# A two-layer hybrid attention encoder on one core: large element-wise operations leave POOL, and PE gets filler matmuls

## The chip, the cores and the metric

The kernel runs on 1 core of one Trainium2 chip. The metric is device time in microseconds (us) of one execution, as the median of the runs shown. The engines are PE (TensorE, matmuls and transposes), ACT (ScalarE), DVE (VectorE), POOL (GpSimd) and SP (which here only issues DMAs).

## The reference, cut to what matters

Two sequences (1024 and 512 tokens, each behind 16 meta tokens) pass through two layers. A layer is a root-mean-square norm, one wide input projection, rotary embedding, a windowed attention (A) with a sink term, a differential attention (B: softmax minus lambda times a second softmax), gates, an output projection, a second norm and the residual add.

```python
h = rmsnorm(x, pre_g)
proj = jnp.einsum('bld,de->ble', h, w_in)            # 1024 -> 3328
aq, ak, av, ag, bq, bk, bv, bg = parts
oa = window_gqa_attention(rope(aq), rope(ak), av, sink) * silu(ag)
ob = diff_attention(rope(bq), rope(bk), bv, lam, lambda_init, subln_g) * silu(bg)
o = jnp.einsum('ble,ed->bld', concat(oa, ob), w_out)  # 1024 -> 1024
return x + rmsnorm(o, post_g)
```

All tensors are float32.

## The kernel before

The 1568 token columns (1040 + 528) stand on the free axis in four chunks of 392 (`CH`), model features on the 128 partitions. A projection (`dense`) multiplies weights and activations that are each split into a rounded part and a rest: three matmuls for each 128 features, so 24 matmuls of up to 392 columns for an output of the input projection. The splitting is what makes so many large element-wise operations: for each weight block `load_w` copies 128x1024 into the rounded half and subtracts to get the rest; `prenorm` does the same for each row of each chunk; `project` does it for rotary results (`st`); `load_mix` does it for the attention results.

The order of the work is planned. Each call of the program is recorded as an operation (`Recorder`, `Engine.form`) with a cost for each engine that may do it, and `schedule` then plays a list schedule: whenever an engine is free it takes the ready operation of the highest priority, subject to buffers (PSUM: `ps_s` 1 buffer, `ps_t` 2, `ps_o` 1, `ps_d` 2). In the plan POOL and those DVE operations that read two SBUF operands exclude each other (`held`). `emit` then issues the operations in the planned order, so that each engine has a fixed queue, and the framework adds the semaphore waits. A planned time is used only for the order.

Where an operation may run on DVE or on POOL it is recorded by `any_tt`: the plan gives it to whichever of the two is free first. These are the weight rests (tile `whl`, also `kk`, `vv`, 128x1024), the prenorm products and rests (`at`, `slot`), the rotary products and sums (`ru`, `rw`, `t`, `st`), the combination of the two softmaxes in attention B (`pp`, up to 1040 columns), the residual adds (`slot`), the sums of squares, and two smaller kinds: the rests of the last 16 keys (`split_rem`, tile `pad`, up to 64 elements) and the gates of attention A (`og`, 256 elements). Three things are on POOL by other calls: the squares of `prestats` with `only=True` (ACT or POOL), the small steps on the statistics (tile `sm`: scale, power -0.5) in `rstd_bc` and `attn_b`, and a memset.

A chunk at the border of two layers goes through `post` (statistics by `rstd_bc`, eight scalings, the residual add, sums of squares) and `pre` (`prenorm` of the next layer), and only then can its next input projection start. `rstd_bc` is PE transpose, DVE sum, two small POOL operations, PE transpose, copy. The last chunk of the last layer ends the kernel with the first half of the same chain.

Of the kernel before, what the change touches and what calls it, by code (L numbers as in the profile page):

```python
# [18 lines left out]
PSUM = bass.MemoryType.PSUM  # L19
# [106 lines left out]
ENG = ("PE", "ACT", "DVE", "POOL", "SP")  # L126
PE_COL = 0.0004453
PE_SWITCH = 0.39


def _size(pat, shape, kw):
# [36 lines left out]
class Buf:  # L168
    def __init__(self, shape, dt, pool, ap=None, space="SB"):
        self.shape, self.dt, self.pool, self.ap, self.space = tuple(shape), dt, pool, ap, space  # L170
        self.acc = []
        self.left = 0
        self.stream = None
        self.live = pool is None
# [55 lines left out]
def _real(x):  # L230
    return x.get() if isinstance(x, View) else x
# [6 lines left out]
class Recorder:  # L238
# [3 lines left out]
    def __init__(self, nc):  # L242
        self.ops = []
        self.group = None
        self.stream = "dense"
        self.boost = 0
        self.base = 0
        self.rnd = random.Random(SEED)
        self.extra = []
        self.last = None  # L250
        self.weight = 1
        self.tensor = Engine(self, "PE", nc.tensor)
        self.vector = Engine(self, "DVE", nc.vector)
        self.scalar = Engine(self, "ACT", nc.scalar)
        self.gpsimd = Engine(self, "POOL", nc.gpsimd)
        self.sync = Engine(self, "SP", nc.sync)
# [37 lines left out]
        return self.call([g[0] for g in got], got[0][1], got[0][2])  # L294

    def any_tt(self, out, a, b, op):
        return self.any((self.vector, "tensor_tensor", (out, a, b), dict(op=op)),
                        (self.gpsimd, "tensor_tensor", (out, a, b), dict(op=op)))

# [138 lines left out]
        return order  # L438

    def emit(self):  # L440
        for o in self.schedule():
            for b in o.new:
                b.ap = b.pool.tile(b.shape, b.dt)
            for fn, args, kw in o.calls:
                fn(*[_real(a) for a in args], **{k: _real(a) for k, a in kw.items()})  # L445


class Pool:
# [9 lines left out]
class Engine:  # L458
# [3 lines left out]
    def form(self, name, args, kw):  # L462
# [14 lines left out]
        elif self.eng == "PE":  # L477
# [10 lines left out]
            if src.shape[0] <= 64:  # L488
                cost += PE_SWITCH
        elif self.eng == "ACT":  # L490
# [46 lines left out]
def hymba_kernel(ctx, tc, xT, w_in, w_out, rope, masks, pre_g, post_g, sub_g, sink_b, sink_m, lam_in, yT):  # L537
    real = tc.nc
    nc = Recorder(real)
# [54 lines left out]
    def f32(ap):  # L594
        return ap.bitcast(F32)
# [25 lines left out]
    identr = const.tile([128, 128], F32R, name="ident")  # L621
    nc.scalar.activation(identr, mk[:, 0:128], AF.Copy)
    ident = f32(identr)
    mhalf = const.tile([128, 4], F32, name="mhalf")
    nc.vector.memset(mhalf, -0.5)
    scl = const.tile([128, 1], F32, name="scl")
# [792 lines left out]
    for i in range(2):  # L1419
        hi, lo = pair(F32R)  # L1420
        for j in range(4):
            g = preg[:, 0, 4 * i + j:4 * i + j + 1]
            x, n = xin[0][i][:, j], CH[0][1]
# [94 lines left out]
```

## Time and profile before

| | us |
|---|---|
| median of 3 runs | 1985.34 (1983.41 to 1994.87) |
| the profiled execution, its own time | 1988.96 |
| its span, first to last instruction | 1986.8 |
| PE busy | 1841.9 (93%) |
| DVE busy | 1509.0 (76%) |
| ACT busy | 1015.0 (51%) |
| POOL busy | 825.2 (42%) |
| mean granted TensorE clock | 0.972 of full |

Busy shares are means over the whole span. What a change is worth is read from the stage it falls in, by what engine is busy there and what the others wait for.

### The profile page before, as it was taken

What the parts mean: (1) busy time and instruction counts of PE and PEld (TensorE: products, weight loads), DVE (VectorE), ACT (ScalarE), POOL (GpSimd) and SP (SyncE); (2) the same over time, 40 slices, a digit from 0 to 9 for tenths busy, and PEclk for the clock granted to TensorE, in tenths of its full rate; (3) what the DMA queues carried; (4) which work ended last, traced back from release to release, by engine and by line L of the source; (5) the groups of instructions that cost most, each with busy time, mean ns of one, the idle gap of its engine ahead of it and who ended that gap; (6) DMA issues with size and microseconds to landing.
All of it is one profiled execution on the core that took longest, in us unless ns stands there. A gap on an engine that the chain in (4) does not pass through costs nothing. (4 is left out here: it accounts for less than half of the span.)

```text
span 1986.8 us, 33503 instructions
## 1 busy us (share of the span) xinstructions
PE 1841.9 (93%) x11424; PEld 1757.3 (88%) x11424; DVE 1509.0 (76%) x3043; ACT 1015.0 (51%) x2358; POOL 825.2 (42%) x833
## 2 busy tenths in 40 slices
PE   5899999999999998999966999999999999899995
PEld 4889989989999988998856999999999998899994
DVE  7858777787777797687986577777877859768768
ACT  3325445454544575576544355555545537547541
POOL 6634362352352351002788452452613513421157
PEclk8999999999999999999978999999999999999997
DMA  6253363443434665555442535445453464764453
GB/s 229 60 159 112 104 169 100 135 128 111 141 93 122 165 176 158 120 134 144 158 151 84 151 98 152 128 128 158 115 173 96 124 166 120 193 176 102 122 173 130
DMA packets 289012, 271.06 MB, mean 136 GB/s; under 512 B 91402, under 2 KB 266058, under 8 KB 288714
## 3 DMA queue, kind: packets, MB, share of 16 engines
q1 hardware_dynamic: 288842, 268.92, 48.1%
q8 instruction: 91, 1.49, 0.3%
q14 instruction: 79, 0.65, 0.1%
HBM read 147.43 MB, written 95.94 MB: 122 GB/s over the span
## 5 line engine op out<-in xcount | busy, mean ns | idle before, releaser
L445 PE MATMUL ps_d<-slot,whl 128*128 128x392 f32 (+2 forms) x5712 | 1180.6, 349 | 53.6 <-POOL slot L445 13.7
L445 PEld LDWEIGHTS ps_d<-slot,whl 128*128 128x128 f32 x5712 | 998.5, 191 | 71.1 <-POOL slot L445 17.1
L445 PE MATMUL ps_s<-kk,qq 128*128 128x264 f32 (+9 forms) x1496 | 286.0, 318 | 18.0 <-DMA BS<-st 4.1
L445 PE MATMUL ps_o<-at,vv 128*128 128x256 f32 (+6 forms) x1368 | 286.3, 308 | 11.1 <-DVE at L445 5.5
L445 DVE TENSOR_TENSOR at<-ps_t,at 128x256 fp32r<-128x256 f32 (+6 forms) x472 | 224.7, 480 | 75.1 <-ACT at L445 67.8
L445 ACT ACTIVATE pp<-ps_s,sm 116x1040 f32<-116x1040 f32 (+4 forms) x208 | 203.9, 980 | 149.2 <-DVE sm L445 138.6
L445 ACT ACTIVATE at<-ps_t 128x256 fp32r<-128x256 f32 (+12 forms) x430 | 183.1, 434 | 166.8 <-PE ps_t L445 153.2
L445 PEld LDWEIGHTS ps_s<-kk,qq 128*128 128x128 f32 (+4 forms) x1496 | 229.1, 184 | 42.0 <-issue 5.2
L445 DVE TENSOR_REDUCE sm<-ps_s 116x1 f32<-116x1040 f32 (+4 forms) x208 | 218.7, 1051 | 51.5 <-PE ps_s L445 48.6
L445 ACT ACTIVATE pp<-pp,sm 128x336 f32<-128x336 f32 (+5 forms) x339 | 201.2, 606 | 77.3 <-DVE sm L445 74.9
L445 PEld LDWEIGHTS ps_o<-at,vv 128*128 128x128 f32 (+1 forms) x1368 | 215.0, 189 | 21.0 <-DVE at L445 9.2
L445 PE MATMUL ps_t<-ident,pp 128*128 128x128 f32 (+4 forms) x1208 | 196.4, 271 | 4.3 <-DVE pp L445 3.1
L445 PEld LDWEIGHTS ps_t<-ident,pp 128*128 128x128 f32 (+4 forms) x1208 | 143.6, 137 | 18.2 <-DVE pp L445 2.9
L445 POOL TENSOR_TENSOR sm<-sm 128x2 f32<-128x2 f32 (+2 forms) x112 | 49.6, 443 | 263.7 <-DVE sm L445 263.1
L445 POOL TENSOR_TENSOR pad<-pp,pad 128x64 fp32r<-128x64 f32 (+5 forms) x121 | 36.2, 302 | 231.3 <-DVE pad L445 117.2
L445 POOL TENSOR_TENSOR pp<-pp 128x1040 f32<-128x1040 f32 (+4 forms) x36 | 75.1, 2085 | 125.3 <-ACT pp L445 125.2
L445 POOL TENSOR_TENSOR whl<-wraw,whl 128x1024 fp32r<-128x1024 f32 x40 | 97.6, 2440 | 64.6 <-ACT whl L445 31.7
L445 POOL TENSOR_TENSOR slot<-slot 128x784 f32<-128x784 f32 (+7 forms) x41 | 93.6, 2286 | 39.3 <-ACT slot L445 14.4
L445 DVE CUSTOM_DVE_ANT_0 pp<-ps_s,mk,nsinks 128x336 f32<-128x336 f32 (+2 forms) x192 | 97.5, 525 | 16.1 <-PE ps_s L445 15.0
L445 POOL TENSOR_TENSOR ru<-ru,rw 128x392 f32<-128x392 f32 (+1 forms) x60 | 66.5, 1112 | 58.4 <-DVE rw L445 47.2
L445 ACT ACTIVATE og<-ps_o 64x128 f32<-64x128 f32 (+4 forms) x248 | 66.0, 287 | 47.6 <-PE ps_o L445 30.4
L445 DVE CAST at<-ps_t 128x256 fp32r<-128x256 f32 (+10 forms) x138 | 70.2, 509 | 16.6 <-PE ps_t L445 12.8
(157 smaller groups left out, 2442.1 us busy)
## 6 DMA issues: line engine op xcount, KB each, us to landing
wraw<-in_w_in_dram SPq DMA_DIRECT2D x48, 512.0 KB
BS<-st SPq DMA_DIRECT2D x112, 196.0 KB
qq<-qq SPq DMA_DIRECT2D x144, 128.0 KB
qq<-AQ SPq DMA_DIRECT2D x96, 128.0 KB
BV<-st SPq DMA_DIRECT2D x28, 392.0 KB
wraw<-in_w_out_dram SPq DMA_DIRECT2D x20, 512.0 KB
slot<-in_x_dram SPq DMA_DIRECT2D x12, 784.0 KB
GT<-ru SPq DMA_DIRECT2D x48, 196.0 KB
```

Source lines behind the costliest of these rows:

```text
L445: fn(*[_real(a) for a in args], **{k: _real(a) for k, a in kw.items()})
```

## The change

`any_tt` gives an operation of more than 300 elements in each partition to DVE alone; smaller ones may still go to either. The plan is made anew from this, so the order on all engines may differ. Second, while it issues, `emit` looks at each PE operation that takes a fresh PSUM buffer: where the plan has PE idle for more than 1.0 us ahead of it, it first issues int((idle - 0.6) / 0.232) matmuls of 512 columns into that buffer, with the identity as weights and one column of the identity, repeated, as the moving operand. Nobody reads their result; the operation that follows overwrites the buffer.

```diff
+POOL_MAX = 300
+FILL_MIN = 1.0
+FILL_REST = 0.6
+FILL_ONE = 0.232
...
     def any_tt(self, out, a, b, op):
+        n = 1
+        for k in out.shape[1:]:
+            n *= k
+        if n > POOL_MAX:
+            return self.vector.tensor_tensor(out, a, b, op=op)
         return self.any((self.vector, "tensor_tensor", (out, a, b), dict(op=op)),
                         (self.gpsimd, "tensor_tensor", (out, a, b), dict(op=op)))
...
     def emit(self):
+        until = 0.0
         for o in self.schedule():
             for b in o.new:
                 b.ap = b.pool.tile(b.shape, b.dt)
+            if o.eng == "PE":
+                fresh = [b for b in o.new if b.space == "PSUM"]
+                if self.filler is not None and fresh:
+                    self.fill(fresh[0], o.t0 - until)
+                until = o.t1
             for fn, args, kw in o.calls:
                 fn(*[_real(a) for a in args], **{k: _real(a) for k, a in kw.items()})
+
+    def fill(self, buf, idle):
+        n = int((idle - FILL_REST) / FILL_ONE) if idle > FILL_MIN else 0
+        out = buf.ap if len(buf.shape) == 2 else buf.ap[:, 0]
+        eye = _real(self.filler)
+        for _ in range(n):
+            self.tensor.raw.matmul(
+                out[:, 0:512], lhsT=eye, rhs=eye[:, 0:1].to_broadcast([128, 512]), start=True, stop=True)
...
     nc.scalar.activation(identr, mk[:, 0:128], AF.Copy)
     ident = f32(identr)
+    nc.filler = identr
```

## Rows read from the trace of the kernel before

**Rows 1.** Busy time of each engine by stage; columns as in the head line.
```profile
core 0: us, PE busy (x) PEld busy (x) DVE busy (x) ACT busy (x) POOL busy (x), PEclk, DMA share, GB/s
0.00:110.00 110.00, 82.18 (x427) 77.06 (x428) 83.93 (x116) 40.11 (x68) 68.26 (x53) 0.92 0.44 138
110.00:950.00 840.00, 805.47 (x5123) 769.87 (x5122) 634.50 (x1403) 449.93 (x1093) 284.61 (x347) 0.99 0.49 133
950.00:1100.00 150.00, 111.64 (x555) 100.49 (x552) 122.89 (x137) 71.01 (x118) 128.43 (x90) 0.85 0.39 131
1100.00:1900.00 800.00, 780.86 (x4985) 752.50 (x4986) 599.40 (x1314) 430.97 (x1037) 289.56 (x305) 1.00 0.51 141
1900.00:1987.00 87.00, 61.72 (x340) 57.41 (x339) 68.26 (x77) 22.94 (x44) 54.34 (x41) 0.88 0.40 133
```

**Rows 2.** Who PE waited for: us in total, times, longest.
```profile
PE ps_t L445 <- POOL sm L445: 16.4, 6, 7.3
...
PE ps_d L445 <- POOL slot L445: 13.7, 8, 3.3
```

**Rows 3.** Groups of POOL, shapes apart: largest and last one over 300 elements.
```profile
L445 POOL TENSOR_TENSOR whl<-wraw,whl 128x1024 fp32r<-128x1024 f32 x40 | 97.6, 2440 | 64.6 <-ACT whl L445 31.7 <-DVE whl L445 29.0 <-DVE sm L445 3.3
...
L445 POOL TENSOR_TENSOR pp<-pp 128x784 fp32r<-128x784 f32 x1 | 2.2, 2205 | 0.0
```

**Rows 4.** Groups of DVE, shapes apart; the first reads PSUM, the others SBUF alone.
```profile
L445 DVE SCALAR_TENSOR_TENSOR ru<-ru,ps_d 128x392 f32<-128x392 f32 x40 | 22.2, 558 | 17.6 <-ACT ru L445 17.4
L445 DVE TENSOR_TENSOR ru<-ru,rw 128x392 f32<-128x392 f32 x30 | 28.7, 955 | 0.5
L445 DVE SCALAR_TENSOR_TENSOR slot<-slot,postg,rb 128x384 f32<-128x384 f32 x16 | 21.6, 1398 | 0.0
```

**Rows 5.** Timeline of DVE and POOL in the border of the layers.
```profile
1001.12 0.96 DVE L445 TENSOR_TENSOR slot<-slot 128x784 f32<-128x784 f32 x1
1004.12 2.88 POOL L445 TENSOR_TENSOR slot<-at,slot 128x392 fp32r<-128x392 f32 x1 [4.36 <-ACT slot L445]
1004.63 0.55 DVE L445 TENSOR_TENSOR t<-t,ru 128x392 f32<-128x392 f32 x1
1005.11 0.55 DVE L445 TENSOR_TENSOR at<-at,rb 128x392 f32<-128x392 f32 x1
1020.75 12.48 DVE L445 SCALAR_TENSOR_TENSOR slot<-slot,postg,rb 128x392 f32<-128x392 f32 x7 [0.30 <-ACT rb L445]
1041.07 0.39 POOL L445 TENSOR_SCALAR sm<-sm 98x4 f32<-98x4 f32 x1
1053.47 4.37 DVE L445 SCALAR_TENSOR_TENSOR slot<-slot,postg,rb 128x392 f32<-128x392 f32 x8
1053.64 5.21 POOL L445 TENSOR_SCALAR sm<-sm 98x4 f32<-98x4 f32 x1 [1.52 <-DVE sm L445]
1060.96 0.91 PE L445 MATMUL ps_t<-ident,sm 98*128 98x98 f32 x4 [7.32 <-POOL sm L445]
```

**Rows 6.** Timeline behind the last dense matmul, DVE and POOL side by side.
```profile
1975.61 2.61 DVE L445 TENSOR_TENSOR slot<-slot 128x384 f32<-128x384 f32 x2
1978.14 4.40 DVE L445 SCALAR_TENSOR_TENSOR slot<-slot,postg,rb 128x384 f32<-128x384 f32 x4
1982.58 1.23 DVE L445 TENSOR_TENSOR slot<-slot 128x384 f32<-128x384 f32 x1
```

**Rows 7.** All 13 stretches at half clock, their first, largest, last and sum; columns as rows 1.
```profile
37.50:51.20 13.70, 6.17 (x20) 5.05 (x21) 10.64 (x15) 3.21 (x6) 8.61 (x6) 0.50 0.18 55
...
1058.10:1075.20 17.10, 7.76 (x23) 6.43 (x24) 5.47 (x5) 7.78 (x12) 15.29 (x13) 0.50 0.26 95
...
1966.10:1986.80 20.70, 1.80 (x6) 1.00 (x6) 14.90 (x14) 0.86 (x2) 12.31 (x11) 0.50 0.39 144
sum 109.70, PE 63.31 PEld 55.98 DVE 70.51 ACT 37.73 POOL 70.23; mean PE 4.87 PEld 4.31 DVE 5.42 ACT 2.90 POOL 5.40
```

More of the change, by code (lines that the diff above doesn't have):

```diff
@@ L251, in __init__ @@
         self.weight = 1
+        self.filler = None
         self.tensor = Engine(self, "PE", nc.tensor)
```

## The prediction

> **What bounds the kernel now.** I read the busy times first: PE is busy 1841.9 us of the span of 1986.8, DVE 1509, POOL 825. A mean can hide a stage, so I cut the span where the work changes [rows 1]. In the two long stretches inside the layers (110 to 950, 1100 to 1900) PE is busy 96% and 98%: PE bounds them, DVE has a quarter of its time free (75 to 76% busy), and a faster side engine buys next to nothing there. At the three edges it is otherwise: the head (0 to 110) has PE busy 75%, the border of the layers (950 to 1100) 74%, the tail (1900 to 1987) 71%. In the border POOL is busy 128 of 150 us and DVE 123: the two side engines set the pace, not PE. The waits of PE say the same: its longest single kind is for the statistics on POOL, followed among others by operations on `slot` on POOL [rows 2]. The clock comes last: 13 stretches of 110 us together were granted 0.5 (1.2 of 2.4 GHz), and PE was busy 63.3 us in them [rows 7]. In each of those I opened, PE had been waiting before or while the clock fell; the largest begins in the wait of 7.32 us at 1053.6 to 1061.0 [rows 5, 7].
>
> **Part one: operations leave POOL.** By the groups of POOL with shapes apart, 375 operations have more than 300 elements in a partition and take 609 us (the first and the last of these groups: [rows 3]). Five at the head are squares that no `any_tt` records and that stay. So 370 move, about 598 us of POOL, some 222,500 elements in each partition. Price on DVE with POOL out of the way: 0.55 us for 392 elements, 0.96 for 784, so (0.96 - 0.55) / 392 = 1.05 ns an element; the next one starts about 0.48 us after the first (1004.63, 1005.11), so some 0.065 us of each is fixed [rows 5]. That makes 222,500 x 1.05 ns + 370 x 0.065 us = 258 us added to DVE.
>
> Against it stands what DVE loses to POOL today. An operation of DVE that reads a PSUM operand takes 558 ns for 392 columns; one that reads SBUF alone takes 955 ns on average, and one kind of 384 columns 1398 ns [rows 4]. In the timeline seven scalings that take 0.55 to 0.62 us alone stretch over 12.48 us, and the reverse is there too: a POOL operation of 392 elements takes 2.88 us while two on DVE run inside it [rows 5]. They take turns, they don't share. I compared every SBUF-only instruction of DVE with the median of its kind and size while POOL rests and summed the excess: 190 us, of which about 185 fall beside operations that move. So DVE becomes 1509 - 185 + 258 = 1582 us, 80% of the span. By stage (same sums): head 84 - 26 + 18 = 76; first long stretch 634 - 37 + 82 = 679 of 840 (81%); border 123 - 43 + 44 = 124; second long stretch 599 - 57 + 94 = 636 of 800 (80%); tail 68 - 24 + 18 = 62. At the edges DVE does POOL's share at no cost at all, and POOL's time on the chain goes.
>
> Border: DVE needs 124 us, PE 111.6, of which 27 are at half clock (would be 99). The busiest engine needs 124 of today's 150, so at most 26 us go. ACT, the transposes and the small POOL steps of the statistics stay in the chain and leave gaps: I take 16 (bounds 0 and 26). Tail: behind the statistics of the last chunk DVE's pieces (2.61 for two additions, 4.40 for four scalings, 1.23 for one addition) [rows 6] run from 1973.9 to 1983.8; with all of POOL's share they would need 4 products and 8 additions at 0.48 and 4 scalings at 0.55, about 7.9 us, so 2 us less. Ahead of that, 1961.9 to 1971, DVE and POOL block each other for another 3: 5 us (bounds 1 and 9). Head: DVE 8 us less, but loads and the first statistics are in the chain: 4 us (bounds 0 and 9). Long stretches: the cover is PE, and DVE rises to 81%. Where PE waits for a result that lies behind a large subtraction in DVE's queue it loses; where it waited for POOL (13.7 us in all for `slot` [rows 2]) it gains. I put this at a loss of 5 us (bounds: gain 15, loss 55; the loss is a rival below).
>
> **Part two: fillers.** Full clock in all 13 stretches would save 63.3 x about half = 30 us of PE at most, and nothing where PE isn't last: in the tail 1.8 us of PE are concerned. Inside the long stretches the share is 24 us, worth 11; in the head 10 us, worth 4, mostly beside a chain of statistics; the border's is in the sum above. Fillers exist only where the plan has a gap, while the trace's gaps partly come from delays that no plan knows: I take 8 us of these 15. Cost: PE is idle 125 us between its instructions, and 41 gaps exceed 1 us, 94 us together, the longest 7.32 [rows 5]. Were the plan's gaps the same, (94 - 41 x 0.6) / 0.232 = 300 fillers would run. One in a gap costs nothing; one that runs when the next operation is ready delays it by its own length, twice that at half clock; and a filler can't start before its PSUM buffer is free, so where the gap is a wait for the buffer it falls behind the gap. Bounds: 0 and 69 us of delay; most gaps at the edges wait for data, not for a buffer, so I take 0 net beyond the 8.
>
> **Sum.** -16 - 5 - 4 + 5 - 8 = -28 us. The profiled execution took 1988.96 us (span plus 2.2), 3.6 above the median of the runs. So 1961 in its terms, 1957 against the median 1985.34.
>
> One rule stands against me. The Trainium skill, "SBUF — State Buffer" (Who interferes with whom), says that POOL and a DVE operation with two SBUF inputs contend for one pair of ports, held for a whole instruction while the other fully blocks. The rows agree: 12.48 us for seven scalings, and 5.21 us for a POOL step that takes 0.39 elsewhere. By that rule the small POOL steps that stay wait longer behind a fuller DVE; this is the second rival, priced from rows.
>
> **Rivals.** (a) The plan has few gaps where the chip has them: no fillers to speak of, the 8 us of clock are missing and part of the border's: 1966. (b) The statistics starve. At 1053.64 a POOL step of 0.39 us lasts 5.21 because eight scalings on DVE run back to back beside it, and PE then waits 7.32 us [rows 5]. Each of the 8 statistics in the border has two such steps; if 4 of the 16 lose 4.8 us on the chain, 19 us of the border's and tail's 21 are gone: 1976. For it: it happens today with POOL full. Against it: DVE's total in the border doesn't rise. (c) Fillers delay: a third of the 69 us falls where operands are ready or buffers late, 23 us: 1980. Against it: the gaps are mostly waits for data. (d) The other side, slower: DVE becomes the bound inside the layers. Some 235 of the moved operations fall there, 0.48 to 1.13 us each (mean 0.75), in a queue served in order, ahead of copies from PSUM of which PE has only two buffers of a kind. If PE sees none, nothing; if it sees 16% of them, the gain of 28 is gone; at 30% it is 53 us: 2010. For it: by the same sums over slices of 50 us, DVE would be busy 46 to 48 us in four of them. Against it: the mean there is 81%, and the plan puts copies ahead by priority. (e) More than the sum: the border shrinks to DVE's 124 us, the tail by 9, the head by 9, PE loses 15 us of waits inside the layers and the clock gives 15: 1985 - 74 = 1911 at the end, 1928 for about three quarters of it.
>
> **How the numbers follow.** About 1% (20 us) is what a measurement of this kernel tells from no change; the three runs shown differ by 0.6%. Chances: forecast 0.56 (its own range 1938 to 1968), (a) 0.10, (b) 0.10, (c) 0.07, (d) 0.07, (e) 0.10. Faster by over 1% (below 1965.5): 0.50 of the forecast, 0.06 of (a), all of (e): 0.66. Slower by over 1%: (d), 0.07. The rest, 0.27, is within 1%. The range runs from 1930, which holds (e) in part, to 1990, which leaves out (d).
>
> **What would show it.** Right: POOL's busy time near 230 us, DVE's near 1580; scalings of 384 columns near 600 ns; the stage between the layers nearer 130 than 150 us; PE waits for `slot` on POOL gone; fewer stretches at half clock; PE instructions above 11424 by some hundreds. Wrong: POOL's statistics still at several us with PE behind them (b), fillers running while the next operands are long done (c), PE waiting for DVE inside the layers at a busy share of DVE near 90% (d).

## The result, and the profile after

The changed kernel took 1967.01 us (median of 4 runs, 1965.23 to 1969.37) against 1987.88 us of the kernel before on the same chip: a ratio of 0.9893, 95% interval 0.9858 to 0.9927. The forecast was 1957 us, 28 us below the median known then; the measured gain is 21 us. The profiled execution has a span of 1967.4 us. Medians here and below leave out four slow executions of the kernels compared, of 2112 to 3605 us.

The page of the changed kernel, its engines and the granted clock in 40 slices:

```profile
PE 1870.9 (95%) x11646; PEld 1778.6 (90%) x11646; DVE 1551.1 (79%) x3384; ACT 1013.7 (52%) x2364; POOL 271.3 (14%) x486
...
PEclk9999999999999999999999999999999999999999
```

222 matmuls are fillers (11646 - 11424). POOL's busy time fell by 554 us and DVE's rose by only 42. The stages of [rows 1] again:

```profile
core 0: us, PE busy (x) PEld busy (x) DVE busy (x) ACT busy (x) POOL busy (x), PEclk, DMA share, GB/s
0.00:110.00 110.00, 100.57 (x549) 94.60 (x550) 83.84 (x154) 42.34 (x70) 20.65 (x22) 1.00 0.54 165
110.00:950.00 840.00, 808.31 (x5157) 768.07 (x5156) 671.10 (x1511) 445.02 (x1096) 123.43 (x250) 1.00 0.49 133
950.00:1100.00 150.00, 129.94 (x691) 119.75 (x690) 127.76 (x216) 71.78 (x119) 26.29 (x18) 0.97 0.44 142
1100.00:1900.00 800.00, 780.33 (x4968) 748.14 (x4967) 615.51 (x1410) 438.74 (x1048) 93.74 (x188) 1.00 0.50 137
1900.00:1987.00 87.00, 51.80 (x288) 48.05 (x286) 52.84 (x95) 15.78 (x32) 7.19 (x8) 0.93 0.38 127
```

Windows at fixed times no longer hold the same work, so I cut both spans at marks: the first score matmul of layer one (on `ps_s`), its last, the first of layer two, the last. From each length I also take the columns that PE's own matmuls stream in it, at the plan's own figure of 0.4453 ns each (`PE_COL`), because the new plan moves dense work from the edges into the layers. "Rest" is what is left of the length. Worked out from the timelines, one profiled execution of each kernel (executions of one kernel differ by up to 4 us after and 13 before, so a difference of 2 or 3 us in one stage is no more than a hint):

```
             before          changed         difference
stage        length  rest    length  rest    length   rest
head          132.8  46.7     117.2  33.7     -15.6  -13.0
layer one     801.8 119.8     814.9 118.3     +13.1   -1.5
border        198.8  69.3     175.4  64.2     -23.4   -5.1
layer two     734.4  88.1     748.3  92.2     +13.9   +4.1
tail          119.1  34.1     111.7  30.3      -7.4   -3.8
```

The groups of DVE that answer to [rows 4], of the changed kernel:

```profile
L461 DVE SCALAR_TENSOR_TENSOR ru<-ru,ps_d 128x392 f32<-128x392 f32 x40 | 22.3, 558 | 13.4 <-ACT ru L461 12.9
...
L461 DVE TENSOR_TENSOR ru<-ru,rw 128x392 f32<-128x392 f32 x80 | 42.9, 556 | 0.0
...
L461 DVE SCALAR_TENSOR_TENSOR slot<-slot,postg,rb 128x384 f32<-128x384 f32 x16 | 9.3, 613 | 0.0
```

The operation that reads PSUM is as long as before, 558 ns. The two that read SBUF alone fell from 955 to 556 and from 1398 to 613. Summed as in the prediction, DVE's excess over its undisturbed lengths fell from 190 to 11 us. Where the last chunk ends, the timeline reads (against [rows 6]):

```profile
1956.43 1.97 DVE L461 TENSOR_TENSOR slot<-slot,rb 128x384 f32<-128x384 f32 x4 [2.37 <-ACT rb L461]
1958.32 1.96 DVE L461 TENSOR_TENSOR slot<-slot 128x384 f32<-128x384 f32 x4
1960.19 2.20 DVE L461 SCALAR_TENSOR_TENSOR slot<-slot,postg,rb 128x384 f32<-128x384 f32 x4
1962.31 1.96 DVE L461 TENSOR_TENSOR slot<-slot 128x384 f32<-128x384 f32 x4
```

Sixteen operations in 7.8 us, with nothing of POOL between them; before, DVE and POOL together needed 9.9.

### The profile page after: what moved, and what is told of

Read it like the earlier page. It is cut to its first block, busy times and chain, and to the rows that moved or that the text cites. A ratio compares the mean times of both kernels' runs of the same rounds, so it can differ in the third digit from the quotient of the medians.

```text
span 1967.4 us, 33819 instructions
## 1 busy us (share of the span) xinstructions
PE 1870.9 (95%) x11646; PEld 1778.6 (90%) x11646; DVE 1551.1 (79%) x3384; ACT 1013.7 (52%) x2364; POOL 271.3 (14%) x486
## 5 line engine op out<-in xcount | busy, mean ns | idle before, releaser
L461 PE MATMUL ps_d<-slot,whl 128*128 128x392 f32 (+2 forms) x5712 | 1165.4, 346 | 16.6 <-DVE slot L461 9.9
L461 PEld LDWEIGHTS ps_d<-slot,whl 128*128 128x128 f32 x5712 | 985.6, 189 | 30.2 <-DVE slot L461 12.9
L461 ACT ACTIVATE at<-ps_t 128x256 fp32r<-128x256 f32 (+9 forms) x435 | 187.7, 440 | 180.4 <-PE ps_t L461 169.2
L461 POOL TENSOR_TENSOR pad<-pp,pad 128x64 fp32r<-128x64 f32 (+3 forms) x143 | 47.2, 332 | 793.3 <-ACT pad L461 494.3
L461 POOL TENSOR_TENSOR sm<-sm 128x2 f32<-128x2 f32 (+3 forms) x112 | 53.1, 475 | 480.7 <-DVE sm L461 467.1
L461 DVE TENSOR_TENSOR slot<-slot 128x784 f32<-128x784 f32 (+8 forms) x74 | 81.5, 1117 | 9.1 <-ACT slot L461 8.8
L461 DVE TENSOR_TENSOR whl<-wraw,whl 128x1024 fp32r<-128x1024 f32 x62 | 76.5, 1234 | 8.3 <-ACT whl L461 7.8
L461 POOL TENSOR_SCALAR sm<-sm 128x2 f32<-128x2 f32 (+6 forms) x72 | 51.8, 719 | 185.5 <-DVE sm L461 180.6
L461 ACT ACTIVATE pad<-pp 128x64 fp32r<-128x64 f32 (+5 forms) x144 | 33.4, 236 | 82.9 <-DVE pp L461 79.2
L461 DVE CAST at<-ps_t 128x256 fp32r<-128x256 f32 (+11 forms) x133 | 65.0, 489 | 12.9 <-PE ps_t L461 10.5
```

## The experiments

**One part alone.** First the new plan without fillers:

```diff
-FILL_MIN = 1.0
+FILL_MIN = 1e9
```

> The plan and the order of the changed kernel, without a single filler. Theory A (the prediction's split, scaled to the 21 us measured): leaving POOL gives about two thirds, fillers one third: about 1974 us. Rival B (the fillers carry the gain, since PE's busy time at half clock fell from 63 to 19 us): about 1984 us, near the kernel before. Rival C (fillers delay real work more than the clock gives back): 1967 us or less.

It took 1969.5 us, ratio 0.9903 (0.9882 to 0.9924), between theory A's 1974 and rival C's 1967. Leaving POOL is nearly the whole gain. The ratio with fillers, 0.9893, lies inside this interval, so whether fillers gain anything in this plan isn't shown. The other half alone, fillers in the plan of before:

```diff
-POOL_MAX = 300
+POOL_MAX = 1000000
```

> The plan and the order of the kernel before, with fillers in its gaps. Theory A: about 1980 us (8 us of clock). Rival B: about 1970 us. Rival C: at or above the 1988 us of before, since the plan that shares work with POOL is the less exact one and its fillers hit ready work.

1993.9 us, ratio 1.0020 (1.0004 to 1.0036): a trifle slower. Theory A's fillers and rival B both fall; C holds in this plan. Since both fillerless kernels issue the same order as their partners, I could follow each matmul through both. In the plan of before, the kernel with fillers gains 4.3 us in the head, loses 9.8 in layer one, gains 3.6 in the border, loses 4.3 in the rest. In the new plan it gains 2.4 in the head and 2.0 in the border and loses 2.7 in layer one. Not all of this is the fillers' doing: of the 9.8 us, some 2.6 are lost at each of two fills (at 405 and 788 us) and stay lost, and the rest builds up between fills.

The clock is not why: it did what was hoped. PE's busy time at half clock, all such stretches together, first the new plan without fillers, then with them:

```profile
sum 86.00, PE 52.91 PEld 48.49 DVE 65.91 ACT 34.21 POOL 14.40; mean PE 4.81 PEld 4.41 DVE 5.99 ACT 3.11 POOL 1.31
```

```profile
sum 29.80, PE 18.82 PEld 17.52 DVE 22.23 ACT 9.17 POOL 5.66; mean PE 3.14 PEld 2.92 DVE 3.71 ACT 1.53 POOL 0.94
```

34 us less of PE at half clock should be worth 17 us; the medians moved by 2.5. Of the 34, 19 lie in the border, where the granted clock of 950 to 1100 rose from 0.86 to 0.97, and 11 in the head; cut at the marks, these two stages became only 4.4 us shorter. What a filler can cost is seen at one place in layer one, here in the changed kernel:

```profile
573.54 1.23 DVE L461 TENSOR_REDUCE sm<-ps_s 116x1 f32<-116x1040 f32 x1
574.80 1.13 ACT L461 ACTIVATE pp<-ps_s,sm 116x1040 f32<-116x1040 f32 x1 [1.78 <-DVE sm L461]
...
576.07 3.42 PE L469 MATMUL ps_s<-ident 128*128 128x512 f32 x8 [2.56 <-ACT pp L461]
```

and in the kernel without fillers:

```profile
575.81 2.08 PE L461 MATMUL ps_s<-kk,qq 128*116 128x264 f32 x6 [2.54 <-ACT pp L461]
```

The gap is a wait for the only `ps_s` buffer, which ACT still reads. Eight fillers wait for that buffer too, start at its end and run 3.42 us, nearly all at half clock (0.50 from 575.6 to 579.0), while the real matmul, ready at 576.1 here and started at 575.8 without them, starts at 579.3. But this loss doesn't last. The kernel with fillers ran 0.2 us behind the other just before this place, 3.5 at it, and 0.5 again at 600: behind the fillers the real work ran at full clock, where without them it was at half (575.2 to 582.1). The lasting part of the 2.7 us came earlier, from 265 to 290 us, where the last filler lay 220 us back. There PE waited 2.00 us for DVE in the changed kernel and the granted clock fell to 0.50 (271.8 to 275.2); without fillers the same wait was 0.23 us and the clock stayed full:

```profile
271.53 2.14 PE L461 MATMUL ps_d<-slot,whl 128*128 128x392 f32 x6 [2.00 <-DVE rw L461]
```

```profile
273.55 1.34 PE L461 MATMUL ps_d<-slot,whl 128*128 128x392 f32 x6 [0.23 <-DVE rw L461]
```

**Some operations alone.** The rule for the edge functions only (`prestats`, `scaled`, `prenorm`, `load_mix`, `squares`, `post` pass `edge=1`), and for all others only (`EDGE = 0`):

```diff
+EDGE = 1
...
-        if n > POOL_MAX:
+        if n > POOL_MAX and edge == EDGE:
```

> Only the operations of the norms, residual adds, squares and attention-result splits leave POOL; weight rests, rotary sums and the softmax combination may go to either. Fillers as in the changed kernel. Theory A (the edges gain, the inside of a layer is PE's): equal to the changed kernel, 1962 to 1970 us. Rival: the weight rests and rotary sums, which are on the chain in the head too, carry half of the gain: 1975 to 1982 us.

> The reverse: only weight rests, rotary sums and the softmax combination leave POOL; norms, residual adds and squares may go to either. Fillers as in the changed kernel. Theory A: the border keeps its time of before (about 10 us longer than in the changed kernel), the inside changes nothing: 1976 to 1982 us. Rival: 1965 to 1972 us.

1991.3 us (1.0013, 0.9995 to 1.0032) and 2015.0 us (1.0118, 1.0085 to 1.0152). Neither expectation holds for either: half of the change gives nothing or costs 24 us, the whole gives 21. The first does have the short tail (111.8 us from the last score matmul, against 111.7 in the changed kernel), but its layer one is 17 us longer beyond its columns than the changed kernel's. I tried fillers as the cause, with the edge functions' rule kept:

```diff
-FILL_MIN = 1.0
+FILL_MIN = 1e9
```

> Only norms, residual adds and squares leave POOL, and no fillers. With fillers the same plan took 1992.2 us, with its border and tail already as short as in the changed kernel but the first layer's inside 15 us longer. Theory A (in a plan that still shares work with POOL the fillers start late and push ready work back): 1974 to 1982 us without them. Rival (sharing inside the layers costs that by itself): 1988 to 1994 us, no change.

1989.9 us, ratio 0.9999 (0.9977 to 1.0020). The rival's time holds: fillers aren't the cause. Whether sharing inside the layers costs it or this particular plan does, the run can't tell.

**Is it the plan?** So I put noise on the priorities, the same on the kernel before and on the changed one without fillers. The lines of the second seed have `SEED = 2`:

```diff
-SEED = 36
+SEED = 1
-SPREAD = 0
+SPREAD = 2
```

> The kernel before with up to 2 steps of random noise on each operation's priority (seed 1), so another plan of the same work. Theory A (the gain comes from POOL's large operations, in whatever plan): 1980 to 2005 us, and the same noise on the kernel without them and without fillers is 12 to 30 us faster than this. Rival B (the plan in use happens to suit the changed kernel; the plans of one kernel differ by as much as the change): plans scatter by over 15 us in either kernel, and one of the two pairs shows no gain.

> The same noise (seed 1) on the changed kernel without fillers. Theory A: 12 to 30 us below its partner. Rival B: between 10 us below and 15 us above its partner.

> As the first, with seed 2. Theory A: 1980 to 2005 us. Rival B: a scatter of over 15 us against seed 1 and against the kernel before.

> Seed 2 on the changed kernel without fillers. Theory A: 12 to 30 us below its partner. Rival B: between 10 us below and 15 us above its partner.

```
                    sharing with POOL      large ones on DVE alone
plan in use         1.0000                 0.9903 (0.9882 to 0.9924)
noise, seed 1       1.0128 (1.0094-1.0163) 0.9938 (0.9922 to 0.9953)
noise, seed 2       1.0183 (1.0159-1.0207) 0.9902 (0.9877 to 0.9927)
```

Both pairs favour the change, by 1.9 and 2.8 points (40 and 54 us of the medians 2022.1 and 1982.1, 2029.4 and 1975.0), more than theory A said. The rival is right in its other half: the kernels that share scatter, over 1.8 points, and the one plan in use is the best of their three. Those that don't share scatter over 0.4. Where the gain falls also depends on the pair. Net of columns, in the order plan in use, seed 1, seed 2 (all without fillers), the border became 3, 10 and 19 us shorter and the tail 4.5, 7 and 12; the two layers together gained 0, 12 and 14; the head gained 11, lost 1.5 and gained 12. The DVE group that showed the turns shows them again, first sharing, then not (seed 2 both):

```profile
L445 DVE TENSOR_TENSOR ru<-ru,rw 128x392 f32<-128x392 f32 x33 | 33.1, 1002 | 0.6
```

```profile
L461 DVE TENSOR_TENSOR ru<-ru,rw 128x392 f32<-128x392 f32 x80 | 42.7, 558 | 0.0
```

**What POOL does to the rest.** Behind each large operation of `any_tt` on DVE, four multiplications of 24 elements on POOL that nobody waits for, or eight memsets of the same tile; no fillers:

```diff
+            if o.moved:
+                scr = _real(self.scratch)
+                for _ in range(4):
+                    self.gpsimd.raw.tensor_tensor(scr, scr, scr, op=ALU.mult)
```

> The changed kernel without fillers (1969.5 us), and behind each of the moved operations POOL is given four small multiplications on a scratch tile (24 elements, two SBUF reads) that nobody waits for. DVE still does all the real work, so no result comes later from POOL's own slowness. Theory A (the ports that DVE and POOL take in turns are what the change won): DVE's SBUF operations get longer again and the time rises by 8 to 20 us, to 1978 to 1990 us. Rival (the gain was only that results no longer wait for a slow POOL): within 4 us of 1969.5.

> The same with eight memsets of the scratch tile in place of the four multiplications: POOL is about as busy and the statistics queue behind it just as much, but it only writes. Theory A: DVE's SBUF operations keep their lengths and the time stays within 6 us of 1969.5, below the run with multiplications. Rival (a fuller POOL queue delays the statistics, ports or not): the same time as the run with multiplications.

2109.7 us (1.0598, 1.0559 to 1.0636) and 2043.7 us (1.0263, 1.0228 to 1.0299). No theory's range holds for either run. The dose was larger than meant: 593 operations carry the mark, since DVE's own share counts too. For the multiplications:

```profile
L467 POOL TENSOR_TENSOR scr<-scr 128x24 f32<-128x24 f32 x2372 | 789.9, 333 | 173.8
```

DVE's excess rose only to 21 us, so turns lost by DVE aren't what costs 140 us. What does for the most part is POOL's queue: a statistics step whose sum on DVE is done stands behind the multiplications.

```profile
1042.82 18.87 POOL L467 TENSOR_TENSOR scr<-scr 128x24 f32<-128x24 f32 x42
1045.26 0.68 DVE L463 TENSOR_REDUCE sm<-ps_t 98x4 f32<-98x512 f32 x1
1061.77 0.19 POOL L463 TENSOR_SCALAR sm<-sm 98x4 f32<-98x4 f32 x1
```

The waits of PE, with multiplications and then with memsets (30.2 us without either):

```profile
PE ps_t L463 <- POOL sm L463: 126.2, 24, 16.4
```

```profile
PE ps_t L463 <- POOL sm L463: 69.9, 17, 14.4
```

These waits grew by 96 us of the 140 and by 40 of the 74. Whatever POOL is given stands ahead of the statistics that PE waits for. In time the pair can't price the turns by themselves, since both of its sides queue. But the lengths of the small operations, sorted by what DVE does meanwhile, show the turns on POOL's side. A multiplication takes 228 ns on average where no DVE operation with two SBUF inputs overlaps it (1646 of them) and 569 ns, up to 5267, where one does (726). A memset, which reads nothing, takes 121 and 120 ns.

**Taking ACT's part out of the norms.**

```diff
-PRE_ACT = ((0, 0, 0, 0, 0, 0, 0, 0), (1, 1, 1, 1, 1, 1, 1, 1))
-POST_ACT = ((0, 0, 0, 0, 0, 0, 0, 0), (1, 0, 1, 0, 1, 0, 1, 0))
+PRE_ACT = ((0, 0, 0, 0, 0, 0, 0, 0), (0, 0, 0, 0, 0, 0, 0, 0))
+POST_ACT = ((0, 0, 0, 0, 0, 0, 0, 0), (0, 0, 0, 0, 0, 0, 0, 0))
```

> The changed kernel with the scalings of the second layer's norms back in one DVE operation instead of a scaling on ACT and a product on DVE (that split served POOL). DVE's own time hardly changes (0.55 against 0.48 us each), one step of ACT of 0.6 us leaves each chain. Theory A (the border and the tail hang on the chain of DVE): 2 to 8 us faster than the changed kernel, 1959 to 1965 us. Rival (DVE is the bound there by its sum): the same or up to 4 us slower.

1978.3 us (0.9939, 0.9918 to 0.9960), 11 us above the changed kernel. Theory A falls. The border grew from 175.4 to 181.2 us with 2 us more of DVE in it, which fits a border bound by DVE's sum but is within what a new plan alone does (by the ratios, seed 1 moved the changed kernel without fillers by 7 us). No version here beats the changed kernel beyond the scatter.

## Why the prediction was right, and where it was not

**The stretches and the price.** Inside the layers PE stayed at 96 to 98% busy, and DVE's 77 to 80% there cost little: beyond their columns the two layers changed by -1.5 and +4.1 us, where I had +5. Rival (d), DVE as the bound inside the layers, did not come. The price of the moved operations was somewhat lower than worked out: DVE's busy time rose by 42 us while its excess fell by 179, so they cost it about 221 us, not 258, and its total is 1551 us, not 1582. One operation of 392 elements takes 556 ns, as in [rows 5]. The Trainium skill, "GPSIMD Engine Reference" (4.1 Engine selection), says that two-input element-wise work takes about twice as long on GpSimd as on VectorE. The traces agree: 2440 ns on POOL for 128x1024 [rows 3], 1234 ns on DVE after.

**They take turns.** The excess of 190 us went to 11, in line with the rule that the prediction took from the Trainium skill, "SBUF — State Buffer" (Who interferes with whom), which has it for POOL instructions that read SBUF. The runs with small operations on POOL agree: multiplications get longer beside DVE, memsets don't. That DVE does POOL's share at the edges for nothing is shown: cut at the marks, DVE was busy 339 us in head, border and tail together before and 320 after, while POOL fell from 296 to 60 (some 24 us of dense columns left these stages too).

**The step that was mis-sized first: fillers.** I put the clock at 8 us and delays at none. The order without fillers took 2.5 us more in the medians, which isn't clear of the noise, and in the plan of before fillers cost 0.2%. PE's time at half clock did go, but in the wrong place: 30 of the 34 us lie in the head and the border, which gained 4.4. Rival (c) was real in small: two fills in the plan of before leave losses of some 2.6 us each. In the new plan the one large delay, 3.3 us at 576, was made good within 25 us.

**The second: the border and the head.** I had 16 us for the border and 4 for the head. Net of columns the border gave 5 and the head 13; the raw border is 23 us shorter mostly because 18 us of dense columns left it, for the layers. That part one as a whole came out at 19 us without fillers (1988.9 to 1969.5), against the 20 that the prediction's terms for it add up to, is luck in part: the border gave too little and the head too much. In the head the first statistics step starts 9.5 us earlier, here before and after; before, POOL worked on weight rests and squares ahead of it:

```profile
32.34 0.19 POOL L445 TENSOR_SCALAR sm<-sm 98x4 f32<-98x4 f32 x1
```

```profile
22.84 1.98 POOL L461 TENSOR_SCALAR sm<-sm 98x4 f32<-98x4 f32 x1 [6.11 <-DVE sm L461]
```

In the border, POOL off the chain wasn't enough: cut at the marks, DVE is busy 146 of 175 us after, against 154 of 199, and PE still waits for the statistics. In the longest gap there, PE waits while DVE works without a pause, and POOL then waits for DVE. The timeline of the new plan without fillers:

```profile
952.42 0.60 PE L461 MATMUL ps_t<-ident,t 128*98 128x128 f32 x4
...
958.92 2.70 DVE L461 SCALAR_TENSOR_TENSOR slot<-slot,postg,rb 128x392 f32<-128x392 f32 x4
...
961.54 1.85 DVE L461 TENSOR_TENSOR slot<-slot 128x784 f32<-128x784 f32 x2
...
963.42 0.69 DVE L461 TENSOR_REDUCE sm<-ps_t 98x4 f32<-98x512 f32 x1
...
964.20 0.44 POOL L461 TENSOR_SCALAR sm<-sm 98x4 f32<-98x4 f32 x1 [4.62 <-DVE sm L461]
964.72 1.40 POOL L461 TENSOR_TENSOR sm<-sm,mhalf 98x4 f32<-98x4 f32 x1
...
966.17 0.92 PE L461 MATMUL ps_t<-ident,sm 98*128 98x98 f32 x4 [10.48 <-POOL sm L461]
```

Of those 10.48 us, eight end in the sum on DVE (963.42 to 964.1). What it sums was there at 953.0, but it stands in DVE's queue behind the scalings and additions of another chunk. This border belongs to the plan in use; with noise on the priorities the same removal made it 10 and 19 us shorter.

**Rival (b) came in part.** The first statistics step of 98x4 elements takes 193 ns at its shortest, 973 ns on average before and 1781 ns after, up to 4.7 us. In the run with multiplications, where it comes late and seldom meets DVE's large operations, it averages 272 ns. The waits of PE for the statistics rose to 30 us without fillers, against 16.4 [rows 2]:

```profile
PE ps_t L461 <- POOL sm L461: 30.2, 9, 10.5
```

So part of what DVE got back is paid by the little that POOL kept: its operations of up to 300 elements took 227 us before and 264 after, and it was busy 271 us, not the 230 named as a sign. **The tail** came as said: from the last dense matmul to the end 23.2 us before, 18.7 after.

**What stays open.** The gain of 19 us by leaving POOL isn't split: how much of it is the end of the turns, and how much that results no longer wait for POOL's slower work, no run separates. Also open is why half of the rule gives nothing: these plans keep 112 and 115 us of DVE's excess (more than half of 190), and are new plans of a kernel that lost 1.3 and 1.8% by the two noisy plans tried. Both are measured; their shares aren't, and each half was run in one plan alone. The measured 21 us are the value of the change against one well-placed plan; against two others the removal from POOL alone is worth 40 and 54 us.

## What to carry to other kernels

Two engines that take turns aren't two engines: sum what the faster loses to the slower, and if that is near the price of doing all of it itself, try moving all of it; the two halves tried here, in one plan each, gave nothing or lost. Filler matmuls raised the clock mostly where PE waited for someone else, so price the clock only by matmuls that are last in their stage. A gap that waits for the very buffer the fillers write can't be filled: they start when the real matmul could. Where a planner fixes the order, repeat a comparison under a little noise on its priorities before a per cent is called the worth of an edit.

## What the runs showed that was not expected

The order that suits one sharing of work is worth as much as the change: up to 2 steps of noise on each priority cost the kernel before 1.3 and 1.8%, the changed one at most 0.4%. And POOL is dear even when nobody waits for its results: multiplications of 24 elements take 333 ns each there (228 out of DVE's way, 569 beside it), memsets of the same tile 121 ns, and in the queue ahead of the statistics they cost 140 and 74 us.
